# Paged attention of a hybrid decoder in steps of four pages, with the prompt bias on TensorE and 44 transfers begun on POOL

## The chip, the cores and the metric

The kernel runs on one core of one Trainium2 chip. The metric is the device time of one execution in microseconds, the median of the runs shown. Engines are called as in the profile: PE (TensorE, matmuls), PEld (its weight loads), DVE (VectorE), ACT (ScalarE), POOL (GpSimd) and SP (SyncE, which here only starts transfers).

## The reference

One step of a two-layer decoder for 512 prompt tokens and 8 samples of 4 tokens each. Every layer projects its input into four groups of mixers, A (short convolution), B (gated DeltaNet), C (HGRN2) and D (differential attention, 4 heads of two 32-wide queries and one 64-wide value), joins them, and applies a SwiGLU (layer 0) or a mixture of experts (layer 1). The change is in D and in the transfers of all four. What D computes, cut to what matters:

```python
for each head h, with the maps m = 1, 2:
    s_m = (q_m @ k_m.T) / sqrt(32) + rel_bias[h, bucket(q_pos - k_pos)]   # causal
    p_m = softmax(s_m)
out = (p_1 - lam * p_2) @ v                                              # then an RMS norm
```

For the prompt, k and v are those of the step itself. A sample's keys and values are 16 pages of 128 past tokens, found through `page_table` in a cache, and its own 4 new tokens. Outputs are the hidden states, the new keys and values, and the states of the convolutions and of B and C.

## The kernel before

The program is written with a framework that lists each engine's instructions in an order of its own at compile time: by priority, which is the order of the program text, and by when an instruction could start. On the chip each engine works through its list in order. Buffers of one name rotate (`bufs=`), and an instruction that needs a buffer waits until its last reader is done.

In `mixers(l, ...)` the order of the text is d_in (queries, keys, values of D), mix_b, `d_attn`, mix_a, mix_c, so attention fills in behind mix_b and stands ahead of mix_c. PSUM has three banks for projections (`st`), three for attention (`dx`) and two for the other mixers (`mx`). All matmuls are issued by a helper `mm` (line 290) and all two-operand vector operations by `tt` (line 293); groups of the profile at these lines are told apart by their tiles. A float32 matmul shows as two passes, each an instruction in the trace.

`d_sample` is a generator. It treats the samples in two groups g of four. A group takes 16 steps; a step loads one page of each of the four samples (`page`, line 616: one 256 KB transfer, K and V side by side, begun on SP into one of nine `kv` buffers). Then come, in one dx bank:

- QK: eight matmuls, the two halves tl of the heads outside, the samples b inside; sample b writes the 32 partitions from 32b (`dx<-kv,qs`)
- the maximum (line 632, DVE), the exponential (line 634, ACT), a transpose (line 635, PE) and its copy `et` (line 637, DVE)
- AV: four matmuls of 256 columns (`dx<-kv,et`)
- `select`: of the four heads' values each row keeps its own, a product (line 293, `r<-dx,cst`) and a sum (line 603), both on DVE, into partial result `pj[:, j]`

After 16 steps the new tokens make partial result 17, and lines 658 to 674 join the 17.

`d_attn` runs one of the 16 prompt heads (`d_head`) after every second step. A head is a block of 128 queries: for each map m scores into a dx bank, the bias added in place on DVE (`dx<-dx,bt`: 48 additions of 256 columns and 16 of 128 in both layers), maximum (692), exponential (694) into a `kv` buffer; then the second map is scaled (699, DVE), both are joined (700), transposed into a third dx bank (703), copied (704, ACT), multiplied with the values and copied out (708, DVE).

mix_c goes through 4 chunks of each of two halves; the last operation of a chunk is the update of its state at line 1177, one for each of two heads. Its first POOL operation (a memset at line 1098) uses memory of mix_b and waits for mix_b's output `gs` to land.

Each layer starts 22 transfers of outputs and states in the mixers on SP, at lines 572, 574, 752, 794, 795, 984, 989, 1069, 1179, 1184, 1228, 1234, 1259 and 1260; some lines start several. Weights (`wraw`, line 364) and pages are also begun on SP, in one order with them.

Of the kernel before, what the change touches and what calls it, by code (L numbers as in the profile page):

```python
# [18 lines left out]
L = 2  # L19
# [20 lines left out]
KVB = 9  # L40
# [146 lines left out]
def _pack(a):  # L187
# [19 lines left out]
    f["kv"] = _cols(np.concatenate([kp, a["cache_v"].reshape(L, npool, 128, 256)], 3))  # L207
# [58 lines left out]
def _body(ctx, tc, I, O):  # L266
# [210 lines left out]
    def mixers(l, y32, hook):  # L477
# [91 lines left out]
        def d_in():  # L569
            q = win_arr("d_q", 32.0 ** -0.5, y32[:, 6:8])  # L570
            k = win_arr("d_k")
            SP.dma_start(O["k"][l].rearrange("a p t -> p a t"), k)
            v = win_arr("d_v")
            SP.dma_start(O["v"][l].rearrange("a p t -> p a t"), v)
# [13 lines left out]
        def d_attn(q, k, vt, qs):  # L588
            heads = [d_head(q, k, vt, qb, tl, h2) for qb in range(4) for tl in range(2) for h2 in range(2)]
            for n, _ in enumerate(d_sample(k, vt, qs)):  # L590
                if n % 2 == 1:
                    heads[n // 2]()
            for i in range(2):
                rms_d(y32[:, 6:8], i, nd[:, l:l + 1])

        def d_sample(k, vt, qs):
            od = y32[:, 6:8]
            ends = []

            def select(pj, po):  # L600
# [4 lines left out]
            regs = []  # L605

            def page(i):
                if i == len(regs):
                    with ExitStack() as qx:
                        if len(ends) > 8:  # L610
                            qx.enter_context(tc.issue_after(ends[-9].ins))
                        _, r = nc.values_load_multi_w_load_instructions(ptb[:, i:i + 8], engines=[mybir.EngineType.SP],
                                                                        min_val=0, max_val=I["kv"].shape[1] - 1)
                    regs.extend(r)
                t = dq.tile([128, 512], F32, name="kv", bufs=KVB)
                ends.append(SP.dma_start(t, I["kv"][l][bass.ds(regs[i], 1)].rearrange("o p f -> p (o f)")))
                return t

            for g in range(2):
                nm = dq.tile([128, 20], F32, name="nm", bufs=2)  # L620
                zz = dq.tile([128, 20], F32, name="zz", bufs=2)
                pj = dq.tile([128, 17, 64], F32, name="pj", bufs=1)
                for j in range(16):
                    kv = [page(64 * g + 4 * j + b) for b in range(4)]
                    ps = dx()
                    for tl in range(2):
                        for b in range(4):
# [444 lines left out]
        def mix_c(bp):  # L1072
# [110 lines left out]
            for i in range(2):  # L1183
                SP.dma_start(s0[i], I["sh"][l][:, i])
# [907 lines left out]
```

## Time and profile before

| | |
|---|---|
| median of 3 runs | 2262.31 us (2260.86 to 2270.95) |
| span of the profiled execution | 2255.7 us |
| instructions in it | 47059 |
| mixers, layer 0 | about 84 to 482 us |
| mixers, layer 1 | about 1040 to 1450 us |

The page of the profile gives busy times and the chain of work that ended last. The time of the profiled execution was not taken apart from its span; the median is 6.6 us above the span. An engine's busy time is the time in which at least one of its instructions runs; of PE's instructions the ends are modelled. Lines (L616 is line 616) are those of the kernel before.

### The profile page before, as it was taken

How to read it: one execution, taken by the hardware profiler on the slowest of the kernel's cores; microseconds unless marked ns; L12 is line 12 of the kernel's file. 1: busy time of each engine (PE TensorE's matmuls, PEld its weight loads, DVE VectorE, ACT ScalarE, POOL GpSimd, SP SyncE). 2: the span in 40 equal slices, each digit the busy share in tenths (PEclk: the TensorE clock that was granted, in tenths of full speed). 3: DMA queues.
4: the chain of work that ended last, by engine and by line, in shares of the span. 5: the costliest groups of instructions: out<-in, count | busy, mean ns of one | idle time of the engine just before them, and what ended most of it. 6: DMA issues, size and time to landing. Idle time of an engine off the chain costs nothing.

```text
span 2255.7 us, 47059 instructions
## 1 busy us (share of the span) xinstructions
PE 2093.5 (93%) x18052; PEld 1843.4 (82%) x18052; DVE 1495.0 (66%) x2944; ACT 820.8 (36%) x1842; POOL 431.1 (19%) x544
## 2 busy tenths in 40 slices
PE   8999899998999999999999999897999998898986
PEld 7976676778999999889777666686889897897875
DVE  4675657767333334746756667568989987777795
ACT  3522425455222223435323345444334433334221
POOL 0100002102000000111000111003514436535431
PEclk9998999989999999999988999798999999999998
DMA  6343434242222323542524343237868786586751
GB/s 235 99 137 119 124 114 142 86 134 94 93 78 84 98 90 103 169 155 90 160 90 129 123 132 96 93 104 243 257 216 284 223 286 203 171 269 206 276 182 60
DMA packets 153490, 340.92 MB, mean 151 GB/s; under 512 B 29411, under 2 KB 39784, under 8 KB 153256
## 3 DMA queue, kind: packets, MB, share of 16 engines
q1 hardware_dynamic: 140840, 324.09, 45.1%
q0 software_dynamic: 3312, 11.60, 1.6%
q10 hardware_dynamic: 9104, 2.13, 0.5%
q8 instruction: 144, 2.36, 0.5%
q14 instruction: 90, 0.74, 0.1%
HBM read 319.91 MB, written 17.85 MB: 150 GB/s over the span
## 4 chain that ended last, share of the span: by engine, by line
PE 66%; DVE 12%; POOL 7%; issue 5%; ACT 4%; DMA 4%; SPq 0%; DVEq 0%; ACTq 0%; POOLq 0%
PE st L290 32%; PE ff L290 12%; PE mx L290 9%; PE dx L290 8%; DVE wl L293 4%; POOL m_g L293 2%; DVE wh L366 2%; PE ee L290 2%; POOL m_u L293 2%; ACT wh L368 1%; POOL hg L293 1%; POOL r L1402 1%; ACT ev L1668 1%; DMA ys_d<-yt 1%; DMA sd<-d 1%
## 5 line engine op out<-in xcount | busy, mean ns | idle before, releaser
L293 DVE TENSOR_TENSOR wl<-wraw,wh 128x1024 fp32r<-128x1024 f32 (+2 forms) x474 | 562.7, 1196 | 283.7 <-ACT wh L368 260.8
L290 PE MATMUL st<-xh,wh 128*128 128x256 f32 (+1 forms) x1536 | 465.0, 303 | 15.5 <-ACT wh L368 11.2
L290 PE MATMUL st<-xl,wh 128*128 128x256 f32 (+1 forms) x1536 | 463.0, 301 | 6.6 <-DVE xl L293 6.5
L290 PE MATMUL st<-xh,wl 128*128 128x256 f32 (+1 forms) x1536 | 462.3, 301 | 1.8 <-DVE wl L293 1.8
L368 ACT ACTIVATE wh<-wraw 128x1024 fp32r<-128x1024 f32 (+2 forms) x280 | 274.1, 980 | 496.3 <-PE st L290 290.1
L290 PEld LDWEIGHTS st<-xh,wh 128*128 128x128 f32 x1536 | 297.7, 194 | 34.2 <-issue 13.1
L290 PEld LDWEIGHTS st<-xh,wl 128*128 128x128 f32 x1536 | 297.8, 194 | 25.6 <-issue 21.4
L290 PEld LDWEIGHTS st<-xl,wh 128*128 128x128 f32 x1536 | 298.2, 194 | 24.8 <-issue 13.9
L290 PE MATMUL st<-xg,wh 128*128 128x416 f32 (+4 forms) x880 | 248.7, 358 | 29.8 <-ACT ev L1668 27.4
L290 PE MATMUL st<-xg,wl 128*128 128x208 f32 (+4 forms) x880 | 215.0, 245 | 3.6 <-DVE wl L293 3.3
L290 PEld LDWEIGHTS st<-xg,wh 128*128 128x128 f32 x880 | 167.1, 190 | 38.9 <-ACT ev L1668 35.7
L290 PEld LDWEIGHTS st<-xg,wl 128*128 128x128 f32 x880 | 169.8, 193 | 8.3 <-DVE wl L293 8.2
L366 DVE CAST wh<-wraw 128x1024 fp32r<-128x1024 f32 (+2 forms) x194 | 159.2, 821 | 16.5 <-PE ee L290 12.1
L290 PE MATMUL st<-hg,wh 128*128 128x416 f32 (+4 forms) x440 | 126.9, 367 | 2.2 <-POOL hg L293 2.2
L1402 POOL TENSOR_SCALAR r<-r,par 128x256 f32<-128x256 f32 (+1 forms) x32 | 29.0, 920 | 487.1 <-ACT xh L1401 487.1
L290 PE MATMUL st<-hg,wl 128*128 128x208 f32 (+4 forms) x440 | 110.0, 250 | 1.6 <-DVE wl L293 1.5
L290 PE MATMUL ff<-hh,wl 128*128 128x256 f32 (+1 forms) x352 | 103.3, 293 | 3.2 <-DVE wl L293 3.2
L290 PE MATMUL st<-wh,xg 128*128 128x256 f32 x528 | 104.1, 291 | 0.0
L290 PE MATMUL ff<-hh,wh 128*128 128x256 f32 (+1 forms) x352 | 103.2, 293 | 1.0 <-ACT wh L368 1.0
L290 PE MATMUL ff<-hl,wh 128*128 128x256 f32 (+1 forms) x352 | 102.1, 290 | 0.0
L290 PE MATMUL ff<-xh,wl 128*128 128x256 f32 (+1 forms) x352 | 101.8, 289 | 0.0
L290 PE MATMUL ff<-xl,wh 128*128 128x256 f32 (+1 forms) x352 | 101.7, 289 | 0.0
(566 smaller groups left out, 4296.8 us busy)
## 6 DMA issues: line engine op xcount, KB each, us to landing
kv<-in_kv_dram SPq DMA_DIRECT2D x256, 256.0 KB, 3.7
wraw<-in_w_in_dram SPq DMA_DIRECT2D x57, 512.0 KB, 4.1
wraw<-in_m_g_dram SPq DMA_DIRECT2D x54, 512.0 KB, 4.5
wraw<-in_m_u_dram SPq DMA_DIRECT2D x54, 512.0 KB, 4.5
wraw<-in_m_g_dram SPq DMA_DIRECT2D x65, 256.0 KB, 4.4
wraw<-in_m_u_dram SPq DMA_DIRECT2D x65, 256.0 KB, 4.7
wraw<-in_w_o_dram SPq DMA_DIRECT2D x32, 512.0 KB, 3.6
wraw<-in_m_d_dram SPq DMA_DIRECT2D x40, 384.0 KB, 3.6
```

Source lines behind the costliest of these rows:

```text
L290: return PE.matmul(out, lhsT, rhs, start=start, stop=stop)
L293: return e.tensor_tensor(out, a, b, op=op)
L366: V.tensor_copy(h, r)
L368: S.activation(h, r, AF.Copy)
L1402: G.tensor_scalar(ri[:, u], ri[:, u], gcol[:, u:u + 1], bcol[:, u:u + 1], op0=OP.mult, op1=OP.add)
L1668: S.activation(t[:, 0:2 * cap], ps[:, 0:2 * cap], AF.Copy)
```

## The change

Attention of the samples works on four pages of each of four samples at a time, so a group has 4 steps instead of 16. K and V lie in two arrays and come in transfers of 128 KB into `pg` buffers of two pages each (seven of them); `kv` buffers go from nine to five. QK has the sample outside and the half inside, with 256 columns for each matmul, and fills the whole bank; one maximum and one exponential treat 512 columns; four transposes follow, and one copy on ACT. AV adds up the four pages in PSUM, so that one `select` follows instead of four. A group has 5 partial results. The new tokens use one dx bank. The prompt heads are now spread over 20 stops of the generator. In a head a matmul of the identity with the bias adds it to the scores in PSUM, the scaling goes from DVE to ACT, and the two score banks are used again for the transposes and the output. The 22 transfers of each layer are begun on POOL (`G`).

```diff
-KVB = 9
+KVB = 5
+PGB = 7
...
-    f["kv"] = _cols(np.concatenate([kp, a["cache_v"].reshape(L, npool, 128, 256)], 3))
+    f["kc"] = _cols(kp)
+    f["vc"] = _cols(a["cache_v"].reshape(L, npool, 128, 256))
...
-            SP.dma_start(O["k"][l].rearrange("a p t -> p a t"), k)
+            G.dma_start(O["k"][l].rearrange("a p t -> p a t"), k)
             v = win_arr("d_v")
-            SP.dma_start(O["v"][l].rearrange("a p t -> p a t"), v)
+            G.dma_start(O["v"][l].rearrange("a p t -> p a t"), v)
...
         def d_attn(q, k, vt, qs):
             heads = [d_head(q, k, vt, qb, tl, h2) for qb in range(4) for tl in range(2) for h2 in range(2)]
+            done = 0
             for n, _ in enumerate(d_sample(k, vt, qs)):
-                if n % 2 == 1:
-                    heads[n // 2]()
+                while done < 16 and done < (n + 1) * 16 / 20:
+                    heads[done]()
+                    done += 1
+            while done < 16:
+                heads[done]()
+                done += 1
...
+            def big(name, n):
+                return dq.tile([128, 512], F32, name="kv", bufs=KVB)[:, 0:n]
...
-            regs = []
-
-            def page(i):
-                if i == len(regs):
+            def indices(i):
+                out = []
+                for o in (0, 8):
                     with ExitStack() as qx:
-                        if len(ends) > 8:
-                            qx.enter_context(tc.issue_after(ends[-9].ins))
-                        _, r = nc.values_load_multi_w_load_instructions(ptb[:, i:i + 8], engines=[mybir.EngineType.SP],
-                                                                        min_val=0, max_val=I["kv"].shape[1] - 1)
-                    regs.extend(r)
-                t = dq.tile([128, 512], F32, name="kv", bufs=KVB)
-                ends.append(SP.dma_start(t, I["kv"][l][bass.ds(regs[i], 1)].rearrange("o p f -> p (o f)")))
-                return t
+                        if len(ends) > PGB:
+                            qx.enter_context(tc.issue_after(ends[-PGB - 1].ins))
+                        _, r = nc.values_load_multi_w_load_instructions(ptb[:, i + o:i + o + 8], engines=[mybir.EngineType.SP],
+                                                                        min_val=0, max_val=I["kc"].shape[1] - 1)
+                    out.extend(r)
+                return out
+
+            def pages(src, regs, u):
+                out = []
+                for b in range(4):
+                    t = dq.tile([128, 2, 256], F32, name="pg", bufs=PGB)
+                    for a in range(2):
+                        ends.append(SP.dma_start(t[:, a], I[src][l][bass.ds(regs[4 * (2 * u + a) + b], 1)].rearrange("o p f -> p (o f)")))
+                    out.append(t)
+                return out
 
             for g in range(2):
-                nm = dq.tile([128, 20], F32, name="nm", bufs=2)
-                zz = dq.tile([128, 20], F32, name="zz", bufs=2)
-                pj = dq.tile([128, 17, 64], F32, name="pj", bufs=1)
-                for j in range(16):
-                    kv = [page(64 * g + 4 * j + b) for b in range(4)]
+                nm = dq.tile([128, 8], F32, name="nm", bufs=2)
+                zz = dq.tile([128, 10], F32, name="zz", bufs=2)
+                pj = dq.tile([128, 5, 64], F32, name="pj", bufs=2)
+
+                def soft(ps, j, n):
+                    V.reduce_max(nm[:, j:j + 1], ps[:, 0:n], axis=AX.X, negate=True)
+                    e = big("e", n)
+                    S.activation(e, ps[:, 0:n], AF.Exp, bias=nm[:, j:j + 1], accum_out=zz[:, j:j + 1])
+                    return e
+
+                for j in range(4):
+                    regs = indices(64 * g + 16 * j)
                     ps = dx()
-                    for tl in range(2):
-                        for b in range(4):
-                            mm(ps[32 * b:32 * b + 32, 0:128], qs[:, tl, 4 * g + b, :], kv[b][:, 128 * tl:128 * tl + 128],
-                               start=tl == 0, stop=tl == 1)
-                    if j == 15:
-                        tt(V, ps[:, 0:128], ps[:, 0:128], bs[:, 0:128], OP.add)
-                    V.reduce_max(nm[:, j:j + 1], ps[:, 0:128], axis=AX.X, negate=True)
-                    e = dq.tile([128, 128], F32, name="e", bufs=3)
-                    S.activation(e, ps[:, 0:128], AF.Exp, bias=nm[:, j:j + 1], accum_out=zz[:, j:j + 1])
-                    PE.transpose(ps[:, 128:256], e, ident)
-                    et = dq.tile([128, 128], F32, name="et", bufs=3)
-                    V.tensor_copy(et, ps[:, 128:256])
-                    for b in range(4):
-                        mm(ps[32 * b:32 * b + 32, 256:512], et[:, 32 * b:32 * b + 32], kv[b][:, 256:512])
-                    select(pj[:, j], ps[:, 256:512])
+                    for u in range(2):
+                        for b, t in enumerate(pages("kc", regs, u)):
+                            for tl in range(2):
+                                mm(ps[32 * b:32 * b + 32, 256 * u:256 * u + 256], qs[:, tl, 4 * g + b, :],
+                                   t[:, :, 128 * tl:128 * tl + 128], start=tl == 0, stop=tl == 1)
+                    if j == 3:
+                        tt(V, ps[:, 384:512], ps[:, 384:512], bs[:, 0:128], OP.add)
+                    e = soft(ps, j, 512)
+                    yield
+                    for a in range(4):
+                        PE.transpose(ps[:, 128 * a:128 * a + 128], e[:, 128 * a:128 * a + 128], ident)
+                    et = big("et", 512)
+                    S.activation(et, ps, AF.Copy)
+                    for u in range(2):
+                        vs = pages("vc", regs, u)
+                        for a in range(2):
+                            for b in range(4):
+                                o = 128 * (2 * u + a) + 32 * b
+                                mm(ps[32 * b:32 * b + 32, 0:256], et[:, o:o + 32], vs[b][:, a], start=2 * u + a == 0, stop=2 * u + a == 3)
+                    select(pj[:, j], ps[:, 0:256])
                     yield
                 ps = dx()
                 for tl in range(2):
                     for b in range(4):
                         mm(ps[32 * b:32 * b + 32, 0:32], qs[:, tl, 4 * g + b, :], k[:, tl, NP_:T], start=tl == 0, stop=tl == 1)
                 tt(V, ps[:, 0:32], ps[:, 0:32], bs[:, 128 + 32 * g:160 + 32 * g], OP.add)
-                V.reduce_max(nm[:, 16:17], ps[:, 0:32], axis=AX.X, negate=True)
-                sn = dq.tile([128, 32], F32, name="sn", bufs=1)
-                S.activation(sn, ps[:, 0:32], AF.Exp, bias=nm[:, 16:17], accum_out=zz[:, 16:17])
-                pe = dx()
-                PE.transpose(pe[0:32, 0:128], sn, ident)
+                sn = soft(ps, 4, 32)
+                PE.transpose(ps[0:32, 0:128], sn, ident)
                 etn = dq.tile([32, 128], F32, name="etn", bufs=1)
-                V.tensor_copy(etn, pe[0:32, 0:128])
-                po = dx()
+                V.tensor_copy(etn, ps[0:32, 0:128])
                 for b in range(4):
-                    mm(po[32 * b:32 * b + 32, 0:256], etn[:, 32 * b:32 * b + 32], vt[0:32, 4, :])
-                select(pj[:, 16], po[:, 0:256])
-                V.tensor_reduce(nm[:, 17:18], nm[:, 0:17], axis=AX.X, op=OP.min)
-                wj = dq.tile([128, 17], F32, name="wj", bufs=1)
-                S.activation(wj, nm[:, 0:17], AF.Exp, bias=nm[:, 17:18], scale=-1.0)
-                tt(V, zz[:, 0:17], zz[:, 0:17], wj, OP.mult)
-                V.tensor_reduce(zz[:, 17:18], zz[:, 0:17], axis=AX.X, op=OP.add)
-                V.reciprocal(zz[:, 17:18], zz[:, 17:18])
-                V.tensor_scalar(zz[:, 18:19], C("m1"), neglam[:, l:l + 1], 1.0, op0=OP.mult, op1=OP.add)
-                V.tensor_scalar(zz[:, 19:20], C("m1"), -1.0, zz[:, 18:19], op0=OP.mult, op1=OP.add)
-                tt(V, zz[:, 17:18], zz[:, 17:18], zz[:, 19:20], OP.mult)
+                    mm(ps[32 * b:32 * b + 32, 0:256], etn[:, 32 * b:32 * b + 32], vt[0:32, 4, :])
+                select(pj[:, 4], ps[:, 0:256])
+                yield
...
-                    mm(ps[:, 0:nk], q[p0:p0 + 32, tl, q0:q0 + 128], k[p0:p0 + 32, tl, 0:nk])
-                    tt(V, ps[:, b0:nk], ps[:, b0:nk], bt[:, h, 256 - (nk - b0):256], OP.add)
+                    mm(ps[:, 0:nk], q[p0:p0 + 32, tl, q0:q0 + 128], k[p0:p0 + 32, tl, 0:nk], stop=False)
+                    mm(ps[:, b0:nk], ident, bt[:, h, 256 - (nk - b0):256], start=False)
...
-                V.tensor_scalar(e[1][:, 0:nk], e[1][:, 0:nk], zz[:, 5:6], None, op0=OP.mult)
+                S.activation(e[1][:, 0:nk], e[1][:, 0:nk], AF.Copy, scale=zz[:, 5:6])
                 V.scalar_tensor_tensor(e[0][:, 0:nk], e[0][:, 0:nk], zz[:, 4:5], e[1][:, 0:nk], op0=OP.mult, op1=OP.add)
-                pw = dx()
+                po, pw = pss
                 for kb in range(qb + 1):
                     PE.transpose(pw[:, kb * 128:(kb + 1) * 128], e[0][:, kb * 128:(kb + 1) * 128], ident)
                 S.activation(e[1][:, 0:nk], pw[:, 0:nk], AF.Copy)
-                po = pss[0]
...
-            SP.dma_start(scb, I["scb"][l])
+            G.dma_start(scb, I["scb"][l])
...
-            SP.dma_start(O["cbp"][l], cstg[:, :, 0:3])
-            SP.dma_start(O["cbs"][l].rearrange("p c b w -> p c (b w)"), cstg[:, :, 3:27])
+            G.dma_start(O["cbp"][l], cstg[:, :, 0:3])
+            G.dma_start(O["cbs"][l].rearrange("p c b w -> p c (b w)"), cstg[:, :, 3:27])
...
-                    SP.dma_start(O["gp"][l, hs(h), i], st[hs(h), 64 * h:64 * h + 64])
+                    G.dma_start(O["gp"][l, hs(h), i], st[hs(h), 64 * h:64 * h + 64])
...
-            SP.dma_start(s0, I["sg"][l])
+            G.dma_start(s0, I["sg"][l])
...
-            SP.dma_start(O["gs"][l], s0)
+            G.dma_start(O["gs"][l], s0)
...
-                    SP.dma_start(O["hp"][l, hs(h), i], st[hs(h), 64 * h:64 * h + 64])
+                    G.dma_start(O["hp"][l, hs(h), i], st[hs(h), 64 * h:64 * h + 64])
...
-                SP.dma_start(s0[i], I["sh"][l][:, i])
+                G.dma_start(s0[i], I["sh"][l][:, i])
...
-                SP.dma_start(O["hs"][l][:, i], s0[i])
+                G.dma_start(O["hs"][l][:, i], s0[i])
...
-            SP.dma_start(sca, I["sca"][l])
+            G.dma_start(sca, I["sca"][l])
...
-            SP.dma_start(O["cap"][l], stg[:, :, 0:2])
-            SP.dma_start(O["cas"][l].rearrange("p c b w -> p c (b w)"), stg[:, :, 2:18])
+            G.dma_start(O["cap"][l], stg[:, :, 0:2])
+            G.dma_start(O["cas"][l].rearrange("p c b w -> p c (b w)"), stg[:, :, 2:18])
```

What is left out here renumbers the columns of `nm` and `zz` in the joining of the partial results, and puts a stop at its end.

## Rows read from the trace of the kernel before

**Rows 1.** The page: span, busy time by engine (part 1), chain that ended last by engine (part 4).

```profile
span 2255.7 us, 47059 instructions
...
PE 2093.5 (93%) x18052; PEld 1843.4 (82%) x18052; DVE 1495.0 (66%) x2944; ACT 820.8 (36%) x1842; POOL 431.1 (19%) x544
...
PE 66%; DVE 12%; POOL 7%; issue 5%; ACT 4%; DMA 4%; SPq 0%; DVEq 0%; ACTq 0%; POOLq 0%
```

**Rows 2.** Windows of the mixers: stretch, its length, busy PE, PEld, DVE, ACT, POOL.

```profile
84.00:338.00 254.00, 239.87 (x2350) 182.11 (x2348) 167.76 (x474) 84.21 (x214) 13.83 (x33) 0.92 0.39 123
338.00:455.00 117.00, 114.95 (x1525) 81.84 (x1526) 84.25 (x225) 57.93 (x180) 28.37 (x55) 1.00 0.36 110
...
sum 808.00, PE 767.79 PEld 568.74 DVE 540.34 ACT 321.29 POOL 88.77; mean PE 127.97 PEld 94.79 DVE 90.06 ACT 53.55 POOL 14.80
```

**Rows 3.** Timeline of PE: start, length, line, operation, shapes, passes.

```profile
82.27 1.18 PE L290 MATMUL mx<-row,cst 128*128 128x256 f32 x4
...
155.38 0.41 PE L290 MATMUL dx<-kv,qs 128*32 128x128 f32 x2
155.71 0.40 PE L290 MATMUL st<-xh,wh 128*128 128x288 f32 x1
...
159.40 0.62 PE L290 MATMUL dx<-kv,qs 128*32 128x128 f32 x10
...
207.91 0.65 PE L290 MATMUL dx<-kv,vt 128*64 128x128 f32 x4
...
301.67 0.87 PE L290 MATMUL dx<-kv,vt 128*64 128x128 f32 x6
```

**Rows 4.** Lines 708 and 1177 from 338 us; DVE's timeline of the latter.

```profile
L708 DVE COPY y<-dx x6: 275/288/294, 351.8 to 443.9; 64x128 f32<-64x128 f32 x6
...
L1177 DVE SCALAR_TENSOR_TENSOR hst<-hst,eb,mx x16: 264/280/288, 375.9 to 462.4; 64x64 f32<-64x64 f32 x16
...
409.15 0.58 DVE L1177 SCALAR_TENSOR_TENSOR hst<-hst,eb,mx 64x64 f32<-64x64 f32 x2
...
455.75 0.57 DVE L1177 SCALAR_TENSOR_TENSOR hst<-hst,eb,mx 64x64 f32<-64x64 f32 x2
...
462.10 0.58 DVE L1177 SCALAR_TENSOR_TENSOR hst<-hst,eb,mx 64x64 f32<-64x64 f32 x2
```

**Rows 5.** Groups by shape, whole span: count, busy us, mean ns, idle before.

```profile
L290 PE MATMUL dx<-kv,qs 128*32 128x128 f32 x1024 | 93.8, 290 | 2.0 <-DMA kv<-in_kv_dram 1.6 <-issue 0.4
...
L290 PE MATMUL dx<-kv,et 128*32 128x256 f32 x512 | 45.7, 400 | 0.5 <-DVE et L637 0.5
...
L603 DVE TENSOR_REDUCE pj<-r 128x64 f32<-128x256 f32 x68 | 40.6, 597 | 0.2
...
L293 DVE TENSOR_TENSOR r<-dx,cst 128x256 f32<-128x256 f32 x68 | 28.5, 420 | 25.0 <-PE dx L290 24.6
...
L293 DVE TENSOR_TENSOR dx<-dx,bt 128x256 f32<-128x256 f32 x48 | 20.6, 430 | 25.9 <-PE dx L290 25.8
...
L635 PE MATMUL dx<-cst,e 128*128 128x128 f32 x64 | 19.1, 305 | 2.7 <-ACT e L634 2.7
...
L637 DVE COPY et<-dx 128x128 f32<-128x128 f32 x64 | 18.0, 285 | 12.2 <-PE dx L635 11.5
```

**Rows 6.** Waits of SP's queue, 84 to 482: us in total, times, longest.

```profile
SPq L616 <- PE dx L290: 75.9, 28, 7.8
...
SPq L1184 <- PE mx L290: 29.9, 1, 29.9
```

**Rows 7.** Waits of POOL, 84 to 482.

```profile
POOL offd L1098 <- DMA out_gs_dram<-lt: 32.9, 1, 32.9
```

**Rows 8.** DMA issues: queue, count, KB each, median us from issue to landing.

```profile
wraw<-in_m_g_dram SPq DMA_DIRECT2D x54, 512.0 KB, 4.5
...
out_gs_dram<-lt SPq DMA_DIRECT2D x2, 512.0 KB, 2.9
...
wraw<-in_m_g_dram POOLq DMA_DIRECT2D x1, 512.0 KB, 8.7
```

More of the change, by code (lines that the diff above doesn't have):

```diff
@@ new lines, in d_sample @@
+                select(pj[:, 4], ps[:, 0:256])
+                yield
+                V.tensor_reduce(nm[:, 5:6], nm[:, 0:5], axis=AX.X, op=OP.min)
+                wj = dq.tile([128, 5], F32, name="wj", bufs=1)
+                S.activation(wj, nm[:, 0:5], AF.Exp, bias=nm[:, 5:6], scale=-1.0)
+                tt(V, zz[:, 0:5], zz[:, 0:5], wj, OP.mult)
+                V.tensor_reduce(zz[:, 5:6], zz[:, 0:5], axis=AX.X, op=OP.add)
+                V.reciprocal(zz[:, 5:6], zz[:, 5:6])
+                V.tensor_scalar(zz[:, 6:7], C("m1"), neglam[:, l:l + 1], 1.0, op0=OP.mult, op1=OP.add)
@@ L667, in d_sample @@
+                V.tensor_scalar(zz[:, 7:8], C("m1"), -1.0, zz[:, 6:7], op0=OP.mult, op1=OP.add)
+                tt(V, zz[:, 5:6], zz[:, 5:6], zz[:, 7:8], OP.mult)
                 tt(V, pj, pj, bc(wj, 64), OP.mult)
@@ L669, in d_sample @@
                 V.tensor_reduce(rd, pj.rearrange("p j v -> p v j"), axis=AX.X, op=OP.add)
-                V.tensor_scalar(rd, rd, zz[:, 17:18], None, op0=OP.mult)
+                V.tensor_scalar(rd, rd, zz[:, 5:6], None, op0=OP.mult)
                 pf = dx()
@@ L674, in d_sample @@
                 V.tensor_copy(od[:, :, NP_ + 16 * g:NP_ + 16 * g + 16], pf[:, 0:32].rearrange("p (a t) -> p a t", a=2))
+                yield
         def d_head(q, k, vt, qb, tl, h2):
```

## Prediction

> **What bounds the kernel now.** I read the page first [rows 1]. The reader is to see that TensorE (PE) is busy for 93% of the span and owns 66% of the chain that ended last; VectorE (DVE) is busy 66% and owns 12%, ScalarE (ACT) 36% and 4%, GpSimd (POOL) 19% and 7%, all DMA 4%. So the change, which takes work from DVE and gives some to PE, has to pay on the engine that is short.
>
> Then the windows, because an average over the span mixes stages [rows 2]. The change touches only the mixer stages of the two layers, three windows each. Of all six (808 us) PE is busy 767.8, so 40.2 us are openly idle, and DVE is busy 540.3. In 338 to 455, attention together with mix_c, PE shows 114.95 of 117 us: on the face of it there is nothing left to win there except by less PE time. But a busy PE in this view contains the time in which one shape of matmul gives way to another, and the modelled end of each matmul. So I read single visits next.
>
> In the PE's timeline one lone QK call (two passes of 128 columns, one page) starts at 155.38 and the next matmul starts at 155.71: 0.33 us for two passes [rows 3]. A pass of 128 columns costs 0.11 us: visits of four and six passes in one column group take 0.65 and 0.87 us, so two more cost 0.22. The rest of the 0.33, 0.11 us, is the change to another shape, and about as much falls on entering; I charge 0.2 us for a visit. When all four samples' pages are there, ten passes take 0.62 us in all: passes into different column groups (32 columns for each sample) run side by side. So what a QK or AV pass costs hangs on which pass stands next to it.
>
> Last, the pace of the stage [rows 4]. Six heads end between 351.8 and 443.9 us: one per 18.4 us. In the same time a chunk of mix_c (its last operation is line 1177; the first chunk ends at 375.9, the fourth at 409.15) takes 33.25/3 = 11.1 us, and when attention is gone 462.10 − 455.75 = 6.35 us. The two hold each other up.
>
> **The change part by part** (both layers; the sum is made against the profiled execution's 2255.7 us span; the median of the runs, 2262.3, is 6.6 us more, which I carry over unchanged).
>
> *QK.* Before: 1,024 passes of 128 columns, 93.8 us busy [rows 5]. After: 512 passes of 256 columns, 0.22 us each, but now written tile by tile, both halves tl of one sample next to each other, into the same column group. If PE finds all four tiles ready, neighbours of different samples still pair: 16 steps × 2 halves u, each ten slots of 0.218 plus 0.2 for the visit, 76 us (−18). If each of the 128 tiles is a visit of its own, as single pages mostly are now [rows 3], it is 128 × (4 × 0.218 + 0.2) = 137 us (+43). Pages still arrive one by one, so I take a value past the middle, **+22**.
>
> Here a rule of the Trainium skill bears ("TensorEngine Tiling (Array Packing)", section Key Properties): tiles operate independently, so that different tiles can load and multiply in parallel, and changing the mode drains the engine. The rows agree with both halves: ten passes of four tiles in 0.62 us, and 0.11 us lost at a change of shape. By the first half the new order would come near the serial end, +43; by the second, fewer visits, near −18.
>
> *AV.* 512 passes of 256 columns before and after; 45.7 us now [rows 5]. All grouped by four samples: 16 steps × (4 × 2 × 0.218 + 0.2) = 31 us (−15). With the first page of each tile alone: some 32 × 5 × 2 × 0.218 = 70 us, and 160 visits at 0.16, 96 us (+50). V pages come after the step's own K pages and have the softmax's time to land, so I stay near the grouped end: **−3**.
>
> *Transposes.* 64 before and after (19.1 us, 305 ns each), now four in a row: 48 changes of shape at 0.11 saved, **−6** (0 to −13).
>
> *Bias of the prompt heads.* 64 additions leave DVE and become matmuls of full depth on PE: 48 of 256 columns, 2 passes × 0.218, and 16 of 128 columns, 2 × 0.109: 24.4 us; by the nearest shape in the trace, four passes of 256 to 288 columns in 1.18 us [rows 3], 28.3 us for the 48 alone. I take **+26**. Nothing hides it: PE is the busy engine.
>
> *What DVE loses.* 48 of 68 selects: 48 × (0.420 + 0.597) = 48.8 us; the copies of et 18.0; the wide bias additions 20.6 [rows 5]. Together 87 of 540 us (narrower forms, the scaling of e[1] and a shorter tail add a little). ACT takes the copies (16 of 512 columns) and the scalings; at 36% it has room. What this gives PE is less: of 40 us idle in the windows a part belongs to waits for ACT, weights and DMA. **−12**, between 0 (PE has other work) and −25.
>
> *Pace.* A step now waits once, not four times, for the round of maximum, exponential, transpose, copy and select, and a head takes two of the three dx banks (po and pw reuse the two score banks) where it took three. If attention stops being what mix_c's chunks wait for, a chunk falls from 11.1 to 6.35 us [rows 4]: 4.75 × 8 chunks = 38 us per layer, 76 for both. But part of the 11.1 is PE's time given to attention, which has grown by 39 us in this sum, so the gain cannot be whole. I take **−50**, bounds −76 and 0. This is the least certain term. Against it: a step now needs eight K tiles of 256 KB with seven buffers, so the first are released only by their own QK; SP waits 75.9 us for PE to release pages already [rows 6].
>
> *DMAs begun on POOL.* 44 transfers leave SP. On SP one of them, the load of line 1184, waits 29.9 us for a buffer that PE releases [rows 6], and all later loads on SP wait with it. On POOL such a wait holds compute. The load cannot stand ahead of the work that releases its buffer, which has POOL operations of its own up to the end, so I don't charge the 29.9 us; the place that can hurt is the first memset of mix_c (line 1098), which waits 32.9 us for out_gs to land [rows 7]. One late landing per layer: 512 KB took 2.9 us from SP, and a weight of 512 KB took 8.7 us from POOL against 4.5 from SP [rows 8]. So 2 × 2 = **+4**, from 0 to 13 (the worst landing in both layers, with a wait on top). For pages, twice as many issues go through SP, which now waits 75.9 us for their buffers [rows 6] and so has the time: nothing.
>
> On this the Trainium skill ("DMA: Bandwidth & Descriptors", section Issuing engines are not separate DMA queues) says that starting transfers from several engines saves only the sequencer's time. If so the move by itself gains nothing, which is what my term says; no row here shows an output begun on POOL.
>
> Sum: 22 − 3 − 6 + 26 − 12 − 50 + 4 = −19 us. 2262.3 − 19 = **2243**.
>
> **The rivals.**
>
> *A, slower: PE is saturated and the serial order decides.* K tiles come singly, each is a visit of four passes in one column group, QK costs +43 and bias +26, and mix_c's chunks don't get shorter, because PE's own time was the reason for 11.1 us. Even with DVE's relief at its bound: 43 − 3 − 6 + 26 − 25 + 0 + 4 = +39, **2301**. For it: 114.95 of 117 us busy. Against: PE's passes in a stage are far fewer than its busy time, as the 0.33 us for 0.22 of passes shows. It decides once more than about half of the 128 K tiles come alone and the chunk stays above 10 us.
>
> *B, much faster:* the tiles come together, and the pace gain is nearly whole in spite of the bias: −18 − 15 − 6 + 26 − 12 − 50 + 0 = −75, **2187**. For it: passes in different groups run side by side at 159.40. Against: most visits now are lone.
>
> *C, no difference:* half the pace gain only, 22 − 3 − 6 + 26 − 12 − 25 + 4 = +6, **2268**: what DVE gives, PE's bias and QK take.
>
> **How the numbers follow.** My forecast 0.36, A 0.30, B 0.16, C 0.18. The point is that of the forecast. The range goes from B, 2185, to a little past A, 2310, and leaves out AV's bad end on top of A and a whole pace gain with grouped QK; those hold less than 2 in 10. The forecast's own range is 2220 to 2255. 0.5% is 11 us, about what runs of this kernel tell from no change (they spread 0.4%). Faster: B and nearly all of the forecast, 0.50; same: C and the rest, 0.20; slower: A, 0.30.
>
> **What would show it.** QK passes of the page steps: 512, with 137 us if alone, 76 if paired. L634 and L603 in 16 and 20 groups instead of 64 and 68. DVE's busy time in the mixers about 87 us lower, PE's dx work some 40 us higher. Heads closer than 18.4 us, chunks of mix_c between 6.35 and 11.1 us while attention runs, and both mixer stages shorter by about 10 us each. The memset's wait for out_gs some 2 us longer. I am wrong if chunks stay at 11 us, if a new wait of SP or PE for page tiles of more than some 10 us per step shows up, or if POOL stands behind a waiting DMA while PE needs it.

## The result and the profile after

The changed kernel took 2283.9 us (median of 8 runs) against 2261.6 (8 runs) for the kernel before: a ratio of 1.0091, 95% interval 1.0063 to 1.012. A second comparison on another chip gave 1.0063 (1.0035 to 1.009). It is slower, by 14 to 21 us, where 2243 was forecast.

The page of the changed kernel, the lines of [rows 1]:

```profile
span 2284.0 us, 46787 instructions
...
PE 2136.6 (94%) x17668; PEld 1863.0 (82%) x17668; DVE 1401.4 (61%) x2640; ACT 828.4 (36%) x1794; POOL 470.3 (21%) x588
...
PE 70%; DVE 9%; POOL 7%; issue 4%; ACT 4%; DMA 4%; SPq 0%; ACTq 0%; DVEq 0%; POOLq 0%
```

DVE lost 93.6 us of work and PE gained 43.1, in a span 28.3 us longer. PE's share of the chain rose from 66% to 70%, DVE's fell from 12% to 9%. TensorE's granted clock does not explain it: its mean over the span was 0.952 in this execution, and 0.953 in the one profiled before. Over all runs it was 0.953 to 0.955 against 0.945 (see the table of the experiments), so it made the changed kernel look better, not worse.

The windows of the two mixer stages, from the first matmul of attention to the last of the other mixers (stretch, length, then busy PE, PEld, DVE, ACT, POOL, granted clock). First the kernel before, cut in the same way, then the changed kernel:

```profile
84.00:479.00 395.00, 377.73 (x4074) 279.23 (x4072) 264.54 (x729) 155.45 (x431) 43.15 (x89) 0.93 0.37 116
1043.00:1444.00 401.00, 383.04 (x4076) 284.30 (x4075) 265.63 (x733) 155.98 (x430) 45.62 (x89) 0.93 0.37 114
sum 796.00, PE 760.77 PEld 563.52 DVE 530.18 ACT 311.43 POOL 88.77; mean PE 380.39 PEld 281.76 DVE 265.09 ACT 155.71 POOL 44.39
```

```profile
84.00:506.00 422.00, 408.00 (x3881) 293.02 (x3874) 219.25 (x580) 158.67 (x408) 57.05 (x107) 0.91 0.39 113
1072.00:1470.00 398.00, 388.04 (x3901) 281.34 (x3900) 221.74 (x590) 161.82 (x413) 59.50 (x107) 0.97 0.41 122
sum 820.00, PE 796.04 PEld 574.36 DVE 440.99 ACT 320.49 POOL 116.55; mean PE 398.02 PEld 287.18 DVE 220.49 ACT 160.25 POOL 58.28
```

The mixers grew by 24 us, PE's busy time in them by 35.3; DVE's fell by 89.2. So both sides of my account of work came out as sums (+39 and −87), and the time followed PE's side. That the +39 was met is in part luck, as its terms were not (below). In this execution all of the growth lies in layer 0 (422 against 395 us, at a granted clock of 0.91 against 0.93); layer 1 took 398 against 401, at 0.97 against 0.93.

Groups by shape of the changed kernel (count, busy us, mean ns, idle before), which answer to [rows 5]:

```profile
L292 PE MATMUL dx<-pg,qs 128*32 128x256 f32 x512 | 100.5, 404 | 1.7 <-DMA pg<-in_kc_dram 1.7
...
L292 PE MATMUL dx<-pg,kv 128*32 128x256 f32 x512 | 61.6, 399 | 3.7 <-DMA pg<-in_vc_dram 3.6
...
L292 PE MATMUL dx<-bt,cst 128*128 128x256 f32 x96 | 36.8, 468 | 0.0
...
L613 DVE TENSOR_REDUCE pj<-r 128x64 f32<-128x256 f32 x20 | 11.9, 594 | 0.2
...
L295 DVE TENSOR_TENSOR r<-dx,cst 128x256 f32<-128x256 f32 x20 | 8.4, 421 | 11.2 <-PE dx L292 11.1
...
L292 PE MATMUL dx<-bt,cst 128*128 128x128 f32 x32 | 7.8, 326 | 0.0
```

QK went from 93.8 to 100.5, AV from 45.7 to 61.6, the bias costs PE 44.6. In PE's timeline most QK visits (57 of 90) are now lone tiles of four serial passes, 1.05 us with their tail at a granted clock of 1.00, with the next matmul 0.98 us after the start (311.63 for the visit at 310.65):

```profile
308.05 1.05 PE L292 MATMUL dx<-pg,qs 128*32 128x256 f32 x4
...
310.65 1.05 PE L292 MATMUL dx<-pg,qs 128*32 128x256 f32 x4
311.63 0.66 PE L292 MATMUL mx<-vb,lt 128*128 128x64 f32 x4
```

The pace, as in [rows 4], in layer 0 (head outputs; mix_c's first scan; ends of chunks):

```profile
L733 DVE COPY y<-dx x16: 273/289/296, 116.6 to 402.7; 64x128 f32<-64x128 f32 x16
...
L1107 DVE TENSOR_TENSOR_SCAN arr<-cst,arr x2: 1273/1490/1706, 379.0 to 381.2; 128x544 f32<-128x544 f32 x2
...
L1202 DVE SCALAR_TENSOR_TENSOR hst<-hst,eb,mx x16: 261/280/289, 436.6 to 491.7; 64x64 f32<-64x64 f32 x16
...
436.62 0.57 DVE L1202 SCALAR_TENSOR_TENSOR hst<-hst,eb,mx 64x64 f32<-64x64 f32 x2 [1.71 <-ACT y L1199]
442.71 0.57 DVE L1202 SCALAR_TENSOR_TENSOR hst<-hst,eb,mx 64x64 f32<-64x64 f32 x2 [0.80 <-ACT y L1199]
```

Attention did get faster: its last head ends at 402.7, 41 us earlier than before. A chunk of mix_c takes 6.1 us. But it takes that because attention is over: mix_c's first chunk ends at 436.6 and not at 375.9, and its scan comes at 379.0; before, the same scan (line 1082) came at 263.5:

```profile
L1082 DVE TENSOR_TENSOR_SCAN arr<-cst,arr x2: 1281/1282/1283, 263.5 to 266.7; 128x544 f32<-128x544 f32 x2
```

The two used to run side by side; now they run one after the other. This order by itself is not the loss: the fastest variant below (0.9867) has it too, with its last head at 378.9 and its chunks from 408.3 to 462.1, where those before end at 462.4 [rows 4]. Heads and chunks of that variant:

```profile
L734 DVE COPY y<-dx x16: 274/289/295, 117.9 to 378.9; 64x128 f32<-64x128 f32 x16
...
L1203 DVE SCALAR_TENSOR_TENSOR hst<-hst,eb,mx x16: 265/280/288, 408.3 to 462.1; 64x64 f32<-64x64 f32 x16
```

### The profile page after: what moved, and what is told of

Read it like the earlier page. It is cut to its first block, busy times and chain, and to the rows that moved or that the text cites. A ratio compares the mean times of both kernels' runs of the same rounds, so it can differ in the third digit from the quotient of the medians.

```text
span 2284.0 us, 46787 instructions
## 1 busy us (share of the span) xinstructions
PE 2136.6 (94%) x17668; PEld 1863.0 (82%) x17668; DVE 1401.4 (61%) x2640; ACT 828.4 (36%) x1794; POOL 470.3 (21%) x588
## 4 chain that ended last, share of the span: by engine, by line
PE 70%; DVE 9%; POOL 7%; issue 4%; ACT 4%; DMA 4%; SPq 0%; ACTq 0%; DVEq 0%; POOLq 0%
PE st L292 34%; PE ff L292 12%; PE dx L292 11%; PE mx L292 9%; DVE wl L295 3%; POOL m_g L295 2%; PE ee L292 2%; POOL m_u L295 2%; DVE wh L368 2%; ACT wh L370 1%; POOL r L1427 1%; POOL hg L295 1%; ACT ev L1693 1%; DMA wraw<-in_m_u_dram 1%; POOL ex L295 1%
## 5 line engine op out<-in xcount | busy, mean ns | idle before, releaser
L292 PE MATMUL dx<-pg,qs 128*32 128x256 f32 x512 | 100.5, 404 | 1.7 <-DMA pg<-in_kc_dram 1.7
```

The source lines that it names most:

```text
L292: return PE.matmul(out, lhsT, rhs, start=start, stop=stop)
```

## The experiments

All ratios are to the kernel before, run on the same chip, with the 95% interval. 0.1% is 2.3 us. "In" and "out" say whether QK's half tl is inside (as changed) or outside.

| steps of four pages | bias on | 44 transfers on | ratio | mean granted clock | estimate at clock 0.950, us |
|---|---|---|---|---|---|
| no | DVE | POOL | 0.9932 (0.9894 to 0.9971) | 0.952 | −5 |
| no | DVE | two loads on POOL | 0.9951 (0.9921 to 0.998) | 0.949 | −3 |
| no | PE | SP | 1.0035 (1.0008 to 1.0062) | 0.949 | +13 |
| in | DVE | SP | 0.9943 (0.9914 to 0.9973) | 0.953 | +2 |
| in | DVE | two loads on POOL | 0.9922 (0.989 to 0.9954) | 0.954 | −3 |
| in | DVE | POOL | 1.0015 (0.9996 to 1.0034) | 0.950 | +12 |
| in | PE | SP | 1.0059 (1.003 to 1.0088) | 0.960 | +39 |
| in | PE | POOL (the change) | 1.0091 and 1.0063 | 0.953 and 0.955 | +28 and +30 |
| out | DVE | SP | 0.9867 (0.9828 to 0.9906) | 0.952 | −20 |
| out | DVE | two loads on POOL | 0.9878 (0.9848 to 0.9909) | 0.954 | −16 |
| out | DVE | POOL | 0.9971 (0.9938 to 1.0004) | 0.942 | −14 |
| out | PE | SP | 0.9954 (0.9922 to 0.9987) | 0.957 | +9 |
| out | PE | POOL | 0.9965 (0.9933 to 0.9998) | 0.953 | +9 |

The clock column is the mean of the granted TensorE clock over the runs, as a part of full speed; the kernel before has 0.945 (0.944 to 0.946 on each of five chips). Within the runs of one kernel the time falls as this clock rises: the variant "out, DVE, POOL" took 2248.3 us at 0.950 and 2278.8 at 0.933. The slope is 0.9 to 2.2 us for each 0.001, 1.7 over all kernels. The last column is an estimate from that slope: the mean time moved to a clock of 0.950, less that of the kernel before (2261.7) moved in the same way. Single runs lie about 3 us from it. The ratio says what a variant does to the time; the estimate says what is left of that when the clocks are made equal. Why the clocks of the variants differ was not tested.

**Bias back on DVE** in the changed kernel:

```diff
-mm(ps[:, 0:nk], q[...], k[...], stop=False)
-mm(ps[:, b0:nk], ident, bt[...], start=False)
+mm(ps[:, 0:nk], q[...], k[...])
+tt(V, ps[:, b0:nk], ps[:, b0:nk], bt[...], OP.add)
```

> The changed kernel (2283.9 us) with the prompt heads' bias added on DVE again; everything else as changed. Theory 1 (TensorE's time sets the mixers): the 128 bias passes stand in PE's order for about 32 us in both layers (64 pairs of 256 columns at 0.5 us), and go away, so 2250 to 2260 us. Theory 2 (weights of the projections stand behind pages on SP, so mix_c starts late): no less than 2278, since nothing on SP's queue changes. Theory 3 (DVE's relief is what the change lives on): 2284 or more, since 25 us of additions return to DVE.

2273.8 us, 1.0015: 11 to 17 us less than the changed kernel (16 to 18 at equal clock). Theory 3 falls; theory 1 has the sign, and about half of the size.

**QK's half outside:**

```diff
-for b, t in enumerate(pages("kc", regs, u)):
-    for tl in range(2):
+ks = pages("kc", regs, u)
+for tl in range(2):
+    for b, t in enumerate(ks):
```

> The changed kernel with QK's loops exchanged: the half tl outside, the sample b inside, so that neighbours lie in different column groups, as before the change. Theory 1 (PE's time): lone tiles cost four passes, 0.98 us, in the changed kernel; with the half outside a late tile's passes of the second half pair with those of the others, so QK's busy time falls from 100 to about 75 us and the time to 2262 to 2275. Theory 2 (order on SP): 2284 or more, since a K tile is now held until the last of the four has come, and pages wait longer for buffers.

2264.3 us, 0.9965: 22 to 28 us less (19 to 21 at equal clock), from an exchange of two loops. Theory 2's fear, K tiles held longer, did not come true.

**Transfers back on SP** (44 times `G.dma_start` to `SP.dma_start`):

> The changed kernel with the 44 output and state transfers begun on SP again. Theory 1 (PE's time): between 2278 and 2288, the move is worth nothing that can be told. Theory 2 (SP's queue is what delays the weights): 2290 or more, since SP gets more to wait for. Rival (POOL holds compute behind its transfers, which start 8.7 us before they land against 2.9 to 4.5): 2270 to 2278.

2283.5 us, 1.0059: no difference from the changed kernel that can be told. By the estimate at equal clock it is 9 to 11 us slower.

**Projection weights begun on POOL** (in `win`, all but attention's):

> The changed kernel with the mixers' projection weights (all but those of attention) begun on POOL instead of SP, so that they don't stand behind the blocks of 16 pages. Theory 2 (SP's order): the gap of 131 us between two weight loads on SP (241 to 372 us) goes, mix_c's scan (first at 378.6 us) comes back towards 263 us, and the time falls to 2255 to 2265. Theory 1 (PE's time): mix_c's scan may come earlier, but the mixers' end moves by less than 8 us, 2276 to 2292.

2275.3 us, 1.0029 (1.0001 to 1.0057). The scan came 8 us earlier in layer 0 counted from the first matmul of attention (288 and 296 us), not 115. Theory 2 falls: it is not SP's order that holds mix_c back.

**The changed kernel again, and both repairs at once:**

> The changed kernel once more, beside the three others on one chip: every theory says 1.005 to 1.012 of before.

> The changed kernel with the bias on DVE and with QK's half outside, both at once. Theory 1 (TensorE's time sets the mixers, and the two costs stand in different passes): the two effects add, 17 + 25 us below the changed kernel, a ratio of 0.985 to 0.993 to before. Rival (one and the same slack: once either is gone, mix_c's late start sets the end): no better than the better of the two alone, 0.994 to 1.000.

1.0063 and 0.9971. In the time the two don't add: with the half outside and the transfers on POOL, 0.9965 with the bias on PE and 0.9971 with it on DVE are the same. But the clocks are not: 0.953 and 0.942. At equal clock the bias on DVE alone is worth 16 to 18 us, the half outside alone 19 to 21, both together 43 to 45: they add, as theory 1 had it, and the rival's one slack is not borne out.

**Parts alone on the kernel before:**

> The kernel before with only the bias of the prompt heads moved to TensorE. Theory 1: 15 to 32 us slower, 1.006 to 1.014. Theory 3 (DVE's relief pays for it): 0.995 to 1.003.

> The kernel before with only the 44 transfers begun on POOL. My term was +4 us, 1.000 to 1.005. If SP's waits for these transfers were what holds up weights and pages, 0.990 to 0.997.

> The kernel before with only the loads of the two sample states (lines 989 and 1184) begun on POOL, the other 38 transfers on SP. If SP's single wait of 29.9 us at line 1184 is what the move of all 44 wins (0.9932), 0.991 to 0.996; if it is the outputs, 0.998 to 1.002.

The bias costs 0.35%, 8 us (13 at equal clock), less than theory 1's least. The move of the transfers gains 0.68%, 15 us, against my +4; two kinds of loads alone, six transfers of 44, bring 0.49%, which can't be told from it. They include the one for which SP waited 29.9 us [rows 6]. Both variants ran at a higher clock than the kernel before (0.952 and 0.949 against 0.945), and at equal clock 5 and 3 us are left. With the two loads gone from SP, SP waits longer for the buffers of the weights instead, here in layer 0 before and with the loads on POOL:

```profile
SPq L364 <- DVE wl L293: 50.4, 5, 18.4
...
SPq L364 <- DVE wl L293: 83.1, 7, 27.6
```

So the wait was real, but that its end is what the time gains is not shown.

**Steps alone** (bias on DVE, transfers on SP):

> The changed kernel with the bias on DVE again and the 44 transfers on SP again: what is left of the change is the step of four pages (with QK's half inside), the two banks of a head and the scaling on ACT. Theory 1 (TensorE's time): QK +14, AV +18, st, mx and transposes about -20: 1.003 to 1.010. Theory 3 (DVE's relief and the pace pay): 0.985 to 0.998.

0.9943: 13 us faster, inside theory 3's range and against theory 1's. QK and AV are 22 us longer than before in its groups (100.9 and 60.2 us busy), and yet PE's busy time in the mixers is 8.2 us less (its sum is shown below): relief, pace and transposes do pay something, some 35 us by the time. Part of that is the clock, 0.953 against 0.945: at equal clock steps alone are 2 us slower than before, and those terms pay some 20 us. The mixers of the two profiled executions are equally long (795 and 796). Against the same with the bias on PE (1.0059) the bias costs 1.16%, 26 us, the very size of its term (37 at equal clock).

**mix_c's projections earlier** (the block under `with tc.high_priority(1500):`), on the changed kernel and on the one with both repairs:

> The changed kernel with the projections of mix_c (from line 1098 to the gate's silu) given priority over attention by 1500 places, so that mix_c's chunks stand earlier in the engines' orders; no work is added or removed. Theory 4 (attention in steps of 16 pages pushes mix_c's start back by some 60 us, and its chain runs alone at the end): mix_c's scan comes before 330 us instead of 378.6, and the time falls to 0.990 to 1.000 of before. Theory 1 (TensorE's time alone): no change beyond 0.3% from the changed kernel's 1.006 to 1.009.

> The variant with the bias on DVE and QK's half outside (0.9971), and mix_c's projections 1500 places earlier as well. Theory 4: 0.980 to 0.992. Theory 1: 0.994 to 1.000.

On the changed kernel 1.0032 (1.0001 to 1.0063). The lines 733, 1108 and 1203 of this kernel are the head output, the scan and the chunk:

```profile
L733 DVE COPY y<-dx x16: 274/289/295, 117.1 to 454.3; 64x128 f32<-64x128 f32 x16
...
L1108 DVE TENSOR_TENSOR_SCAN arr<-cst,arr x2: 1274/1274/1275, 279.8 to 281.3; 128x544 f32<-128x544 f32 x2
...
L1203 DVE SCALAR_TENSOR_TENSOR hst<-hst,eb,mx x16: 264/280/287, 386.8 to 476.3; 64x64 f32<-64x64 f32 x16
```

The order did what was asked: the scan 99 us earlier, the first chunk 50. But attention's last head now ends at 454.3, 52 us later, and the time fell by 0.3 to 0.6% only. What one side gains in PE's order the other loses. With both repairs it gave 0.9885 (0.9836 to 0.9934), 0.86% below 0.9971 and inside theory 4's range; of these 20 us the clock (0.948 against 0.942) makes all but 7.

**Half outside with the transfers on SP**, then with the projections earlier, with the two loads on POOL, and with the bias on PE:

> Steps of four pages alone (bias on DVE, the 44 transfers on SP; 0.9943) with QK's half outside, the sample inside. If the order of the passes is worth the same whatever else stands in PE's order, 0.983 to 0.990; if mix_c's late start sets the end here, 0.992 to 0.997.

> The same with mix_c's projections 1500 places earlier. Theory 4 (mix_c's start is what is left): 0.978 to 0.986; otherwise as the variant without it.

> Steps of four pages alone (0.9943) with only the loads of the two sample states begun on POOL. If these loads in POOL's order are what cost the changed kernel something beside the bias (1.0015 with all 44 moved): 0.999 to 1.003. If it is the other transfers or the order of the list: 0.991 to 0.997.

> Steps of four pages with the half outside and transfers on SP (0.9867), and the bias on TensorE. If the bias costs what it cost with the half inside (1.16% of the time of before): 0.996 to 1.001. If its price hangs on how full PE's order is with serial QK passes, 0.986 to 0.992.

> Steps of four pages with the half outside, bias on DVE, and only the two loads of the sample states begun on POOL. The loads gained 0.5% on the kernel before and 0.2% on the steps: 0.982 to 0.987. If they gain nothing once SP isn't short: 0.985 to 0.990.

0.9867, 0.9899, 0.9922 (this one with the half inside), 0.9954 and 0.9878. The first is the best version found: 2234.8 us, 33 us under the kernel before. Earlier projections bring nothing here. The loads on POOL bring nothing that can be told on top of steps, and don't hurt. The bias costs 0.87%, 20 us (29 at equal clock), between the two ranges and nearer to the first.

QK of this best version, its busy time and two visits:

```profile
L292 PE MATMUL dx<-pg,qs 128*32 128x256 f32 x512 | 74.6, 411 | 4.3 <-DMA pg<-in_kc_dram 4.3
...
245.75 1.02 PE L292 MATMUL dx<-pg,qs 128*32 128x256 f32 x10
...
269.07 0.64 PE L292 MATMUL dx<-pg,qs 128*32 128x256 f32 x8
```

The same passes at the same granted clock of 1.00: 8 in 0.64 us, 10 in 1.02, where the changed kernel's four took 1.05. QK's busy time is 26 us less than with the half inside (100.9), the time 17 us less, 22 at equal clock.

**The bias added twice:**

> The changed kernel with the matmul that adds the bias done twice, so the bias counts twice in the scores; it adds 128 passes to PE's order and nothing to another engine. Theory 1 (a pass of the bias costs its time on PE in full): 24 to 32 us more than the changed kernel, 1.017 to 1.023 of before. Theory 2 (the price of the move is a wait or an order, not the passes): 1.005 to 1.012.

2289.8 us, 1.0094 (1.0061 to 1.0127): 0 to 0.3% above the changed kernel, far under 24 to 32 us. Its clock is again higher (0.959); at equal clock it stands 44 us above the kernel before and 14 to 16 above the changed one. By its groups the bias passes took 75.4 us busy instead of 44.6:

```profile
L292 PE MATMUL dx<-pg,qs 128*32 128x256 f32 x512 | 96.6, 408 | 0.6 <-DMA pg<-in_kc_dram 0.6
...
L292 PE MATMUL dx<-bt,cst 128*128 128x256 f32 x192 | 61.1, 425 | 0.0
L292 PE MATMUL dx<-pg,kv 128*32 128x256 f32 x512 | 56.9, 405 | 5.7 <-DMA pg<-in_vc_dram 5.7
L292 PE MATMUL dx<-bt,cst 128*128 128x128 f32 x64 | 14.3, 336 | 0.0
```

Theory 1 in its simple form, a pass costs its own time in full, falls here: 30.8 us more of bias passes, but QK and AV took 8.6 less, and at equal clock the time grew by about half of the passes' busy time. The windows of the mixers of four of these kernels, cut as above: steps alone; steps with the bias on PE; half outside; bias twice.

```profile
86.00:477.00 391.00, 373.29 (x3828) 273.66 (x3827) 230.02 (x616) 161.34 (x411) 42.83 (x89) 0.95 0.44 123
1041.00:1445.00 404.00, 379.25 (x3829) 276.15 (x3828) 230.91 (x622) 160.58 (x410) 41.55 (x89) 0.93 0.43 120
sum 795.00, PE 752.54 PEld 549.81 DVE 460.93 ACT 321.92 POOL 84.38; mean PE 376.27 PEld 274.90 DVE 230.47 ACT 160.96 POOL 42.19
```

```profile
84.00:494.00 410.00, 393.60 (x3897) 282.91 (x3897) 219.89 (x583) 161.64 (x411) 44.37 (x89) 0.97 0.41 118
1061.00:1477.00 416.00, 398.64 (x3897) 287.60 (x3895) 224.66 (x590) 161.65 (x411) 47.00 (x89) 0.94 0.40 117
sum 826.00, PE 792.24 PEld 570.52 DVE 444.55 ACT 323.30 POOL 91.36; mean PE 396.12 PEld 285.26 DVE 222.28 ACT 161.65 POOL 45.68
```

```profile
86.00:478.00 392.00, 364.18 (x3824) 264.93 (x3816) 230.95 (x616) 160.66 (x410) 43.35 (x89) 0.93 0.45 122
1039.00:1428.00 389.00, 370.15 (x3829) 270.95 (x3828) 229.50 (x623) 162.52 (x411) 42.70 (x89) 0.93 0.44 124
sum 781.00, PE 734.33 PEld 535.88 DVE 460.44 ACT 323.18 POOL 86.05; mean PE 367.17 PEld 267.94 DVE 230.22 ACT 161.59 POOL 43.03
```

```profile
84.00:499.00 415.00, 400.25 (x3957) 292.72 (x3956) 226.97 (x584) 160.48 (x410) 59.18 (x107) 0.96 0.40 116
1064.00:1481.00 417.00, 407.11 (x3956) 297.34 (x3947) 226.83 (x591) 160.56 (x409) 58.51 (x107) 0.94 0.39 116
sum 832.00, PE 807.36 PEld 590.06 DVE 453.80 ACT 321.04 POOL 117.70; mean PE 403.68 PEld 295.03 DVE 226.90 ACT 160.52 POOL 58.85
```

With the kernel before (761 of 796) and the changed one (796 of 820), these are six. By PE's busy time they stand 734, 753, 761, 792, 796, 807, by length 781, 795, 796, 826, 820, 832: the same order but for one neighbouring pair. PE is busy for 94 to 97% of each, so the length goes with PE's busy time, which here holds the low clock and the changes of shape as well as the passes. DVE's busy time, in the same order 460, 461, 530, 445, 441 and 454, shows no such order. A second profiled execution of the changed kernel has mixers of 833 us, so the lengths of single executions differ by some 13 us with the clock. Each stretch's length times its granted clock, an estimate of the mixers at full clock, is in the same order 726, 747, 740, 789, 770 and 790: steps alone 7 above the kernel before, the bias 42 on top of them, the half outside 21 below.

## Why the prediction was wrong

**The step that failed is "Pace"**, with "What DVE loses" beside it. Together with the transposes they took 68 us off. The terms of the steps alone (QK, AV, transposes, relief, pace) summed to −49 us; steps alone measured −13. That is 36 of the 41 us by which the forecast missed. QK and AV had 19 us in that sum and show 22 of busy time, so what is left for relief, pace and transposes is −35, half of their terms (about −20 at equal clock). I read the 11.1 us of a chunk under attention against 6.35 us without it as a delay that faster attention would give back. What fits the traces is that two stages shared one full PE. The chunk did fall to 6.1 us, but no chunk ran under attention any more: the last head's end came 41 us earlier, and mix_c's first chunk 61 us later. I had seen PE busy for 114.95 of 117 us [rows 2] and argued it away with the switches between shapes, which left room for a gain that no row showed. Forcing the overlap back by priority gave at most 0.6% on the changed kernel, and the fastest variant does without the overlap: most of the loss is not this order but what stands in it, the bias passes and the serial QK passes. How the missing gain divides between pace and relief stays open.

**QK**: the term of +22 was mis-sized as a busy time (+6.7), but the mechanism was right: beside the order that it could have had it costs about its term, 26 us of busy time (100.9 against 74.6). In time the half inside costs 0.76% (17 us; steps alone), 0.44% (10 us; with the two loads or all transfers on POOL) and 1.0 to 1.26% (22 to 28 us; with the bias on PE as well); at equal clock 13 to 30 us. Rival A named this place.

**AV**: −3 was wrong, 45.7 became 61.6 us. The forecast held that V pages would be there; in one step of PE's timeline (326.74 to 333.88 us) its 32 passes come in visits of 2, 16, 2, 2 and 10, with other work between.

**Transposes** can't be read alone, their terms are small.

**Bias on PE**: +26 had the right sign and mechanism, and its price depends on the company. With the transfers on SP it is 1.16% (26 us) with the half inside and 0.87% (20 us) with it outside; with them on POOL, as in the changed kernel, 11 to 17 us, and nothing with the half outside; on the kernel before 8 us. Doubling it cost at most 7. Much of this spread is the clock: in all five pairs the kernel with the bias on PE had the higher mean granted clock, by 0.003 to 0.011. At equal clock the prices are 37, 29, 16 to 18, 24 and 13 us, and 14 to 16 for the doubling, against 44.6 us of busy time. So by this estimate the passes are paid in every pair, but not at the number of passes times their time. That taking the bias out of the list changes how the scheduler packs attention, and with it how late mix_c starts, fits the scans (in layer 0 at 320.1 us with steps alone, at 346.5 us with the bias on PE), but is argued, not shown.

**What DVE loses**: the work was right (89.2 us less, 87 forecast). Its worth can't be told from the pace's; the six sums above don't follow it.

**Transfers on POOL**: +4 had the wrong sign on the kernel before (−15 us), where I had not charged SP's 29.9 us at line 1184. In the changed kernel the move cost 0 to 0.3% with the bias on PE, but 0.7% (half inside) and 1.0% (outside) with it on DVE. Part of these differences is the clock, and most of it with the half outside. With the half outside and the bias on DVE, runs at 0.945 took 2249.6 us with the transfers on SP and 2255.1 and 2257.5 with them on POOL, and at 0.949 and 0.950 they took 2246.6 and 2248.3. At equal clock the move is worth −5 us on the kernel before, +10 and +6 with steps and the bias on DVE, −9 to −11 and 0 with it on PE: no sign that holds. What moves the clock, and which wait makes the rest, stays open. The feared price of a late landing was too high: 512 KB of `gs` landed 3.9 us after its issue on POOL, against 2.9 from SP [rows 8] and the 8.7 that I took as the bound. That bound came from one load; in the run with the weights begun on POOL, 46 loads of 512 KB landed in 4.1 us.

```profile
out_gs_dram<-lt POOLq DMA_DIRECT2D x2, 512.0 KB, 3.9
```

The Trainium skill ("DMA: Bandwidth & Descriptors", section Issuing engines are not separate DMA queues) says that several issuing engines save only the sequencer's time. In the kernel before that time held a wait of 29.9 us of one load for its buffer, with SP's later issues behind it; what its end is worth is not shown, as said above.

**The account as a whole**: steps −13, bias +26, transfers +1 to +7. These three are the stations of one way from the kernel before to the changed one, so they add up to the measured +14 and +21 by themselves, and that is no test of the terms. At equal clock the stations are +2, +37 and −9 to −11.

## What to carry to other kernels

Where an engine shows 98% in a stage, as PE here, a shorter wait on another engine may only move work about in its order: count what the change adds to the full engine first, and take a gain from pace only if a row shows that engine idle. When matmuls fill a quarter of the columns each, write the loop that changes the column group innermost: the exchange of two loops was worth as much here (10 to 28 us) as the steps of four pages themselves (13 us), and more at equal clock (13 to 30 us, where the steps alone gain nothing). Test the parts of a change alone and together: here two of three gained by themselves (0.9943 and 0.9932), together they gave 1.0015, and with the third 1.0063 to 1.0091. And compare the granted clocks before you give a difference of 1% to a queue or an order: 0.010 of clock went with some 17 us here, as much as most of the parts.

## What the runs showed that I had not expected

Eight QK passes of 256 columns in four column groups take 0.64 us, and four passes in one group take 1.05 us, both at a granted clock of 1.00: lone visits cost 3.3 times as much for each pass. The kernels compared here have mean granted clocks from 0.942 to 0.960, over 6 to 12 runs each, and the one with more matmuls can have the higher clock: moving the bias to PE raised it in five pairs of five. Six loads moved off SP's queue, one of which had waited 29.9 us there, go with a time 0.5% lower, of which about 0.1% is left at equal clock.
